# Conditioning tiles in the norm gaps of a four-layer trunk: ordered behind the last product and dealt out anew, with another order of the first inputs

## The chip, the cores and the metric

The kernel runs on one core of a Trainium2 chip. The metric is the device time of one execution in microseconds (us); the time given for a kernel is the median of several runs.

## The reference: what is computed

A decoder trunk of four layers over 256 tokens of width 1024 in float32. Each layer has a token mixer (layers 0 and 3: gMLP; layer 1: latent attention, MLA; layer 2: HGRN2, a gated linear recurrence) and a causal depthwise-convolution feed-forward network. Both are wrapped in adaptive norms whose shift, scale and gate come from one conditioning vector `c`:

```python
c_act = jax.nn.silu(c)
for i in range(DEPTH):
    mod = c_act @ ada_w[i] + ada_b[i]
    sh1, sc1, g1, sh2, sc2, g2 = jnp.split(mod, 6, axis=-1)
    h = modulate(rmsnorm(x, mix_norm_g[i]), sh1, sc1)
    ...
    x = x + (1.0 + g1)[:, None, :] * y
    h = modulate(rmsnorm(x, ffn_norm_g[i]), sh2, sc2)
    x = x + (1.0 + g2)[:, None, :] * conv_ffn(h, ff_w_up[i], ff_conv_w[i], ff_conv_b[i], ff_w_down[i])
return rmsnorm(x, final_g)
```

## The kernel before

**Products.** All weights stream from HBM in tiles of 1 MB (`raw`, five buffers, issued on SyncE's queue, SP). ScalarE (ACT) casts each half of a tile to a rounded part `wh` (L210), VectorE (DVE) takes the rest `wl` (L213), and TensorE (PE) makes three matmuls for each product (L243 to L245): high times high, and two cross terms. The activations are split likewise into `hh` and `hlo` (L599, L600).

**Stages.** Each layer runs a mixer (`mix`; in the gMLP its parts are `v`, `u` and `go`, in the HGRN mixer the projections, the levels `lev` and the output part `hout` that ends in the product `wo`), then `up` and `dn` of the feed-forward network. Between two stages lies a norm gap, eight in all, counted here from 0: gap 0 is go to up of layer 0, gap 1 is dn of layer 0 to the MLA mixer, gap 2 MLA's wo to up of layer 1, gap 3 dn to the HGRN mixer, gap 4 HGRN's wo to up of layer 2, gap 5 dn to the gMLP of layer 3, gap 6 its go to up. In a gap the last products go through the gate and the residual (`gated`, `x`: L522, L523, with the gate broadcast in `gx`), the root of the squares (`ss`, ACT, then a reciprocal on DVE, L459), the scaling (`gx`, L467 to L470), 16 transposes on PE (`xt`, L478), and the modulation on DVE (`nt`, L487, with the scale in `amul` and the shift in `mod`); only then can the next stage's first product run.

**Conditioning.** The six vectors of each layer, `mod`, are units (layer, u) with u = 0 to 5 for shift, scale and gate of the mixer norm, then of the feed-forward norm. Each unit is four tiles of 1 MB. Units in the list `ADA_P` are made on PE (`adaps`, L324: eight matmuls a tile, 16 records in the trace, since each is recorded twice), units in `ADA_D` on DVE (`adaw`, L349: two reductions over 128x1024 a tile). Units (0,0) and (0,1) come first, column by column (`adaf`, L371).

**What sets the order.** Every engine runs its instructions in the order in which the program's recording layer put them. The table `RATE` gives, for each stage, how many p and d tiles are loaded for every weight tile used; `pacing` (L413) runs a tile two weight tiles after its load. In the last `GAPW` = 7 weight tiles of a stage no p tile is run; up to `GAPS[gap]` of them are kept for the gap, where `modulated` (L491) runs them after the first transposes have been recorded. `need(l, u)` (L406) is the backstop: at a gap it runs, at once and in order, every tile up to the unit that the norm needs, whatever is left of it; `gate_load` (L278) calls it for the gate units, and then sends the gate through DRAM (`gate<-grow`, four small transfers) to be broadcast (`gx<-gate`). With `issue_after` the code holds one instruction behind another in the recorded order; `state["chain"]` does that for the casts and conditioning steps that must not come ahead of the root.

**The start.** x (two halves) goes first on SP's queue, `cin` (the conditioning vector) first on ACT's; twelve warm-up matmuls of 128x128 run on PE; then the first conditioning column `adaf`, the first transposes `xt`, and the products `v` column by column, in the order of the string `FIRST`.

## Time and profile before

| | |
|---|---|
| median of three runs | 1352.13 us (1352.03 to 1352.72) |
| profiled execution | 1353.27 us, of which the span of the trace 1351.2 us |
| mean granted clock of PE | 0.993 |
| PE busy | 1316.6 us, 97% |
| DVE busy | 1112.7 us, 82% |
| ACT busy | 773.5 us, 57% |
| moved by DMA | 330.68 MB, 245 GB/s mean |

Times in the trace are us from the start of the span. A timeline's row gives start, duration, engine, line of the kernel, operation, output and inputs, shapes, and in brackets the idle time of the engine just before, with what ended it. Matmuls are pipelined, so that the durations of neighbours overlap: start to start is what counts. In a window's row the last three columns are the granted clock (1.00 is full), the share of the 16 DMA engines, and GB/s.

### The profile page before, as it was taken

Reading aid. Unit: us, or ns where it says so; the run is one execution under the profiler, and the core shown is the slowest. Engines: PE = TensorE matmul, PEld = TensorE weight load, DVE = VectorE, ACT = ScalarE, POOL = GpSimd, SP = SyncE. Lnnn points to the kernel's source line nnn. Section 1 sums busy time; section 2 is a strip of 40 time slices with the busy share of each in tenths; the row PEclk is TensorE's granted clock in tenths of the full one; section 3 lists DMA queues with packets and bytes.
Section 4 is the critical chain, followed back from the end, with each engine's and each line's share of the span. In section 5 each row is a group of like instructions: output and inputs, shape, how many; then the busy total and the mean of one; then the engine's idle time right before and its main releaser. Section 6 shows DMA issues by size and latency. Waiting matters only on the chain.

```text
span 1351.2 us, 24627 instructions
## 1 busy us (share of the span) xinstructions
PE 1316.6 (97%) x10092; PEld 1192.5 (88%) x10092; DVE 1112.7 (82%) x1818; ACT 773.5 (57%) x1212; POOL 17.3 (1%) x27
## 2 busy tenths in 40 slices
PE   8999989999989999999999999999999999999997
PEld 6799789998777799998897879999878998899986
DVE  5699788888888789999889988988985964888854
ACT  3764366665366566654675647665455644666643
POOL 0100000000000000000000000000001000000000
PEclk8999999999999999999999999999999999999999
DMA  9868945557986466498675575558977445254550
GB/s 378 349 235 318 403 185 187 213 193 267 424 333 244 172 219 244 166 360 359 236 295 190 219 305 189 214 192 317 369 297 259 168 166 216 98 204 179 198 197 32
DMA packets 49160, 330.68 MB, mean 245 GB/s; under 512 B 6548, under 2 KB 7572, under 8 KB 10134
## 3 DMA queue, kind: packets, MB, share of 16 engines
q1 hardware_dynamic: 47888, 327.40, 63.7%
q10 hardware_dynamic: 1160, 1.71, 0.4%
q8 instruction: 79, 1.29, 0.4%
q14 instruction: 33, 0.27, 0.1%
HBM read 328.01 MB, written 1.08 MB: 244 GB/s over the span
## 4 chain that ended last, share of the span: by engine, by line
PE 85%; DVE 9%; ACT 3%; issue 1%; DMA 1%; ACTq 0%; DVEq 0%
PE up L245 12%; PE up L243 12%; PE up L244 12%; PE dn L243 5%; PE dn L245 5%; PE dn L244 5%; PE u L244 2%; PE u L243 2%; PE u L245 2%; DVE wl L213 2%; PE v L243 2%; PE v L244 2%; PE v L245 2%; PE go L243 2%; PE go L244 2%; PE go L245 2%
## 5 line engine op out<-in xcount | busy, mean ns | idle before, releaser
L210 ACT CAST wh<-raw 128x1024 fp32r<-128x1024 f32 x418 | 432.8, 1048 | 324.0 <-PE up L244 110.9
L213 DVE TENSOR_TENSOR wl<-raw,wh 128x1024 fp32r<-128x1024 f32 x418 | 507.2, 1225 | 84.6 <-ACT wh L210 83.8
L245 PE MATMUL up<-hh,wl 128*128 128x256 f32 x1408 | 397.8, 283 | 0.9 <-DVE wl L213 0.9
L243 PE MATMUL up<-hh,wh 128*128 128x256 f32 x1408 | 397.7, 284 | 0.0
L244 PE MATMUL up<-hlo,wh 128*128 128x256 f32 x1408 | 397.3, 283 | 0.1
L245 PEld LDWEIGHTS up<-hh,wl 128*128 128x128 f32 x1408 | 270.4, 192 | 1.3 <-DVE wl L213 1.3
L243 PEld LDWEIGHTS up<-hh,wh 128*128 128x128 f32 x1408 | 270.0, 192 | 0.6 <-issue 0.4
L244 PEld LDWEIGHTS up<-hlo,wh 128*128 128x128 f32 x1408 | 270.1, 192 | 0.3 <-DVE hlo L600 0.3
L349 DVE CUSTOM_DVE_ANT_0 adaw<-adaw,cbc,prm 128x1024 f32<-128x1024 f32 x120 | 151.3, 1282 | 0.3 <-DMA adaw<-adad 0.3
L244 PE MATMUL dn<-wl,gh 128*128 128x512 f32 x352 | 137.0, 389 | 0.0
L245 PE MATMUL dn<-wh,gl 128*128 128x512 f32 x352 | 136.8, 389 | 0.0
L243 PE MATMUL dn<-wh,gh 128*128 128x512 f32 x352 | 134.7, 390 | 0.5 <-DVE y L1217 0.5
L1215 ACT ACTIVATE y<-up,cwb 128x256 f32<-128x256 f32 x176 | 99.0, 562 | 58.1 <-DVE y L1217 57.9
L1216 DVE SCALAR_TENSOR_TENSOR y<-up,cwb,y 128x255 f32<-128x255 f32 x176 | 84.5, 480 | 34.0 <-ACT y L1215 33.5
L1217 DVE SCALAR_TENSOR_TENSOR y<-up,cwb,y 128x254 f32<-128x254 f32 x176 | 84.1, 478 | 1.5
L243 PEld LDWEIGHTS dn<-wh,gh 128*128 128x128 f32 x352 | 66.0, 188 | 15.2 <-issue 1.7
L245 PEld LDWEIGHTS dn<-wh,gl 128*128 128x128 f32 x352 | 66.1, 188 | 13.7
L244 PEld LDWEIGHTS dn<-wl,gh 128*128 128x128 f32 x352 | 66.1, 188 | 13.5
L243 PE MATMUL u<-hh,wh 128*128 128x256 f32 x256 | 74.0, 289 | 0.0
L245 PE MATMUL u<-hh,wl 128*128 128x256 f32 x256 | 72.4, 283 | 0.0
L244 PE MATMUL u<-hlo,wh 128*128 128x256 f32 x256 | 72.4, 283 | 0.0
L600 DVE TENSOR_TENSOR gl<-g,gh 128x256 fp32r<-128x256 f32 x88 | 37.1, 421 | 22.1 <-ACT gh L599 20.5
(332 smaller groups left out, 2060.4 us busy)
## 6 DMA issues: line engine op xcount, KB each, us to landing
raw<-up SPq DMA_DIRECT2D x88, 1024.0 KB
adaw<-adad SPq DMA_DIRECT2D x60, 1024.0 KB
raw<-dn SPq DMA_DIRECT2D x44, 1024.0 KB
adaw<-adap SPq DMA_DIRECT2D x28, 1024.0 KB
raw<-gmu SPq DMA_DIRECT2D x16, 1024.0 KB
raw<-gmo SPq DMA_DIRECT2D x16, 1024.0 KB
raw<-gmv SPq DMA_DIRECT2D x15, 1024.0 KB
adaf<-ada SPq DMA_DIRECT2D x8, 1024.0 KB
```

What stands on the lines that cost most here:

```text
L210: act.copy(wh[:, :w], raw[:, o : o + w])
L213: i = dve.tensor_tensor(wl[:, :w], raw[:, o : o + w], wh[:, :w].bitcast(F32), op=ALU.subtract)
L243: pe.matmul(ps, lh, rh, start=start, stop=False)
L244: pe.matmul(ps, lh, rl, start=False, stop=False)
L245: i = pe.matmul(ps, ll, rh, start=False, stop=stop)
L349: r = dve.tensor_tensor_reduce(raw[:, e, :], raw[:, e, :], cbc[:], 1.0, prm[:, c0 : c0 + 1], ALU.mult, ALU.add, mod[:, l, b : b + 1])
L600: b = dve.tensor_tensor(lo, src, h.bitcast(F32), op=ALU.subtract)
L1215: act.activation(y[:], ps[:, e, :], AF.Identity, bias=b, scale=w[2])
L1216: dve.scalar_tensor_tensor(y[:, 1:], ps[:, e, : S - 1], w[1], y[:, 1:], op0=ALU.mult, op1=ALU.add)
L1217: dve.scalar_tensor_tensor(y[:, 2:], ps[:, e, : S - 2], w[0], y[:, 2:], op0=ALU.mult, op1=ALU.add)
```

## The change

- **Deal.** The tables: `GAPS`, the number of p tiles for MLA (`MLA_ADA` 6 to 2), unit (3,2) from PE to DVE, and the rates. In layer 2 the d rates fall to 0.1, 0.0 and 0.1 in mix, lev and hout; in layer 3 they rise in mix, u and go and fall to 0 in dn.
- **Order in a gap.** In `modulated` the p tiles are held behind the last product matmul (`state["behind"]`).
- **Start.** 22 warm-up matmuls in place of 12, five more behind the first transposes; `cin` first on SP, one half of x on ACT's queue; the first `adaf` tile in two transfers; the squares of the two halves of x on the other engine each; the second half of the first weight tile is cast after hh, and the first `wl` taken after the first nt.
- **End.** The second output half is split at 640 of 1024 columns in place of 512.

```diff
-GAPS = [3, 2, 4, 3, 5, 3, 3, 0]
+GAPS = [3, 3, 3, 3, 2, 2, 2, 0]
...
-WARM = 12
+WARM = 22
+WARM2 = 5
...
-MLA_ADA = 6
+MLA_ADA = 2
...
-ADA_P = [(0, 5), (1, 2), (1, 3), (2, 4), (2, 5), (3, 2), (3, 5)]
+ADA_P = [(0, 5), (1, 2), (1, 3), (2, 4), (2, 5), (3, 5)]
...
-        ("mix", 2): (0.0, 0.4), ("lev", 2): (0.0, 0.25), ("hout", 2): (0.25, 1.05), ("up", 2): (0.0, 0.15),
+        ("mix", 2): (0.0, 0.1), ("lev", 2): (0.0, 0.0), ("hout", 2): (0.25, 0.1), ("up", 2): (0.0, 0.15),
...
     for t in range(2):
-        nc.sync.dma_start(x[:, t, :], A["x"][:, t, :])
-    cin = one.tile([P, 8], F32, name="cin")
-    nc.scalar.dma_start(cin[:], A["c"])
+        (nc.sync if t else nc.scalar).dma_start(x[:, t, :], A["x"][:, t, :])
...
+            if n == 0 and o and "first" in state:
+                es.enter_context(tc.issue_after(state["first"][1]))
             act.copy(wh[:, :w], raw[:, o : o + w])
-            if "sub1" in state:
-                es.enter_context(tc.issue_after(state["sub1"]))
+            if n == 0 and "first" in state:
+                es.enter_context(tc.issue_after(state["first"][0]))
             i = dve.tensor_tensor(wl[:, :w], raw[:, o : o + w], wh[:, :w].bitcast(F32), op=ALU.subtract)
...
-                for k in range(2):
-                    kc = 2 * i + k
-                    for j in range(4):
-                        pe.matmul(ps[32 * j : 32 * j + 32, :], crep(kc), raw[:, k, j, :], start=kc == 0, stop=kc == KC - 1,
-                                  tile_position=(0, 32 * j))
+                with contextlib.ExitStack() as es:
+                    for ins in state["behind"]:
+                        es.enter_context(tc.issue_after(ins))
+                    for k in range(2):
+                        kc = 2 * i + k
+                        for j in range(4):
+                            pe.matmul(ps[32 * j : 32 * j + 32, :], crep(kc), raw[:, k, j, :], start=kc == 0, stop=kc == KC - 1,
+                                      tile_position=(0, 32 * j))
...
         xts = [turned(*i) for i in tiles[:3]]
+        state["behind"] = (state["mm"],)
         while loaded["p"]:
             ada_run("p")
         need(l, 1 + 3 * which)
+        state["behind"] = ()
...
+    def warm(n):
+        for i in range(n):
+            r = pe.matmul(adaps[:, 0, 0:P], onesw[:], onesw[:], start=True, stop=True)
+        return getattr(r, "ins", r)
+
+    warm(WARM)
...
-                                state.setdefault("sub1", modulate_chunk(l, 0, c, xt[0][:, c % 2, :])[0])
+                                ins = modulate_chunk(l, 0, c, xt[0][:, c % 2, :])
+                                if c == 0:
+                                    state["first"] = ins
+                                    with tc.issue_after(state["xt"]):
+                                        firsts["pe"] = warm(WARM2)
```

**Gap 0 on PE.** Ahead of the change PE had the three conditioning tiles (`adaw_5_0` to `adaw_5_2`, unit (0,5)) among the last products `go` of layer 0. Where they begin:

```order
L245 MATMUL go_1503<-wh_1024_1666,yl_869 128x512
L324 MATMUL adaps<-adaw_5_0_1514,cact 32x256 x8
L324 MATMUL adaps<-adaw_5_1_1556,cact 32x256 x8
L324 MATMUL adaps<-adaw_5_2_1594,cact 32x256
L243 MATMUL go_1500<-wh_0_1698,yh_868 128x512
L243 MATMUL go_1501<-wh_0_1698,yh_868 128x512
```

With the change, the end of go:

```order
L248 MATMUL go_1518<-wh_1024_1753,yl_884 128x512
L330 MATMUL adaps<-adaw_5_0_1529,cact 32x256 x8
L330 MATMUL adaps<-adaw_5_1_1571,cact 32x256 x8
L330 MATMUL adaps<-adaw_5_2_1609,cact 32x256 x8
L488 MATMUL xt<-ident,gx 128x128 x16
L246 MATMUL up_1946<-hh,wh_0_1774 128x256
```

All 24 conditioning matmuls have moved from among the products, of which 48 still followed, to between the last product and the transposes.

**Gap 4 on DVE.** Before, from the root of the second token half to the modulation of up's first columns (layer 2):

```order
L459 RECIPROCAL ss<-ss 128x1
L469 TENSOR_SCALAR gx<-x,ss 128x512
L487 TENSOR_SCALAR nt<-xt,amul,mod 128x256 x2
L600 TENSOR_TENSOR hlo<-nt,hh 128x256
L487 TENSOR_SCALAR nt<-xt,amul,mod 128x256
```

The same place with the change; `adaw_3_0` to `adaw_3_3` are the four tiles of unit (2,3), the shift of this norm, and each pair of rows of `adaw` and `mod` is one reduction and the reading of its sum:

```order
L469 RECIPROCAL ss<-ss 128x1
L355 ISA adaw_3_0_8871,mod<-adaw_3_0_8871,cbc,prm 128x1024
L355 ISA mod 128x1
L479 TENSOR_SCALAR gx<-x,ss 128x512
L355 ISA adaw_3_0_8871,mod<-adaw_3_0_8871,cbc,prm 128x1024
L355 ISA mod 128x1
L355 ISA adaw_3_1_8875,mod<-adaw_3_1_8875,cbc,prm 128x1024
...
L355 ISA adaw_3_3_8883,mod<-adaw_3_3_8883,cbc,prm 128x1024
L355 ISA mod 128x1
L498 TENSOR_SCALAR nt<-xt,amul,mod 128x256 x2
L615 TENSOR_TENSOR hlo<-nt,hh 128x256
```

Eight reductions stand between the root and the first nt; before, they were done in the HGRN mixer.

**The gate of the HGRN residual on SP.** Before, SP sent the gate row of unit (2,2) (`gate20`) between two weight tiles of the projections, and the broadcast `gx_8794` much later. With the change both stand at the end of the output part, behind two tiles of up and four or five of conditioning:

```order
L346 DMA adaw2_2_3_8730<-adad 128x2048
L189 DMA raw119_8746<-up 128x2048
L189 DMA raw120_8780<-up 128x2048
L346 DMA adaw2_3_0_8871<-adad 128x2048
L316 DMA adaw2_5_1_8644<-adap 128x2048
L316 DMA adaw2_5_2_8696<-adap 128x2048
L346 DMA adaw2_3_1_8875<-adad 128x2048
L278 DMA gate20_8739<-grow_8737 8x32 x4
L346 DMA adaw2_3_2_8879<-adad 128x2048
L292 DMA gx_8744<-gate20_8739 128x1024
```

The last tile of unit (2,2) itself, `adaw2_2_3`, now comes only ahead of these.

More of the change, by code (lines that the diff above doesn't have):

```diff
@@ L46 @@
 HOLD = (3, 4)
-ADA_P = [(0, 5), (1, 2), (1, 3), (2, 4), (2, 5), (3, 2), (3, 5)]
+ADA_P = [(0, 5), (1, 2), (1, 3), (2, 4), (2, 5), (3, 5)]
 ADA_D = [(0, 2), (0, 3), (0, 4), (1, 0), (1, 1), (1, 4), (1, 5), (2, 0), (2, 1), (2, 2), (2, 3), (3, 0), (3, 1),
-         (3, 3), (3, 4)]
+         (3, 2), (3, 3), (3, 4)]
 RATE = {("mix", 0): (0.05, 0.4), ("u", 0): (0.1, 0.9), ("go", 0): (0.35, 0.7), ("up", 0): (0.05, 0.05),
-        ("dn", 0): (0.0, 0.87), ("mix", 1): (1.85, 0.6), ("up", 1): (0.0, 0.2), ("dn", 1): (0.0, 0.93),
-        ("mix", 2): (0.0, 0.4), ("lev", 2): (0.0, 0.25), ("hout", 2): (0.25, 1.05), ("up", 2): (0.0, 0.15),
-        ("dn", 2): (0.0, 1.09), ("mix", 3): (0.0, 0.5), ("u", 3): (0.0, 0.3), ("go", 3): (0.0, 0.5),
-        ("up", 3): (0.35, 0.0), ("dn", 3): (0.0, 0.76)}
+        ("dn", 0): (0.0, 0.87), ("mix", 1): (1.05, 0.6), ("up", 1): (0.0, 0.2), ("dn", 1): (0.0, 0.93),
+        ("mix", 2): (0.0, 0.1), ("lev", 2): (0.0, 0.0), ("hout", 2): (0.25, 0.1), ("up", 2): (0.0, 0.15),
+        ("dn", 2): (0.0, 0.5), ("mix", 3): (0.0, 0.6), ("u", 3): (0.0, 0.5), ("go", 3): (0.0, 0.7),
+        ("up", 3): (0.0, 0.0), ("dn", 3): (0.0, 0.0)}
 MAGIC = 12582912.0
@@ L125, in build @@
     prm = one.tile([P, NPRM], F32, name="prm")
+    cin = one.tile([P, 8], F32, name="cin")
+    nc.sync.dma_start(cin[:], A["c"])
     for t in range(2):
-        nc.sync.dma_start(x[:, t, :], A["x"][:, t, :])
-    cin = one.tile([P, 8], F32, name="cin")
-    nc.scalar.dma_start(cin[:], A["c"])
+        (nc.sync if t else nc.scalar).dma_start(x[:, t, :], A["x"][:, t, :])
     ident = one.tile([P, P], F32, name="ident")
@@ L171, in want @@
         plan.extend(aps)
-    state = {"dma": 0, "conv": 0, "use": 0, "ahead": 2, "chain": (), "left": 99, "tag": "raw", "p": 0.0, "d": 0.0, "gap": 0, "rate": {"p": 0.0, "d": 0.0}}
+    state = {"dma": 0, "conv": 0, "use": 0, "ahead": 2, "chain": (), "behind": (), "left": 99, "tag": "raw", "p": 0.0, "d": 0.0, "gap": 0, "rate": {"p": 0.0, "d": 0.0}}
     raws = []
@@ L363, in ada_first @@
         raw = wp.tile([P, KC, 4, 64], F32, tag="raw", name=f"adaf{c}", bufs=NRAW)
-        nc.sync.dma_start(raw[:].rearrange("p a b c -> p (a b c)"), A["ada0"][l, c])
+        rawf = raw[:].rearrange("p a b c -> p (a b c)")
+        for o in (0, 1024) if c == 0 else ():
+            nc.sync.dma_start(rawf[:, o : o + 1024], A["ada0"][l, c, :, o : o + 1024])
+        if c:
+            nc.sync.dma_start(rawf, A["ada0"][l, c])
         ps = misc(f"adaf{c}", (P, 64))
@@ L477, in turned @@
             for t in range(2):
-                pe.transpose(ps[:, e, t * P : t * P + P], cur["gx"][:, t, (c + e) * P : (c + e) * P + P], ident[:])
+                i = pe.transpose(ps[:, e, t * P : t * P + P], cur["gx"][:, t, (c + e) * P : (c + e) * P + P], ident[:])
+        state["xt"] = getattr(i, "ins", i)
         return ps
@@ L546, in finish @@
             s = slice(512 * f, 512 * f + 512)
+            if t:
+                s = slice(640 * f, 640 + 384 * f)
             if t == 0:
@@ L1250, in build @@
         act.activation(cbc[:], cbc[:], AF.Silu)
-    warm = misc("warmup", (P, P))
-    for i in range(WARM):
-        pe.matmul(warm[:], onesw[:], onesw[:], start=True, stop=True)
+    def warm(n):
[3 more added lines that the diff above has]
+    warm(WARM)
     cur["gx"] = big("gx", (P, 2, D))
@@ L1258, in build @@
         act.activation(sm("warm", 1)[:], epsc[:], AF.Sqrt)
-    act.activation(sq0[:, 0, :], x[:, 0, :], AF.Square, accum_out=ss0[:, 0:1])
-    dve.tensor_tensor_reduce(sq0[:, 1, :], x[:, 1, :], x[:, 1, :], 1.0, 0.0, ALU.mult, ALU.add, ss0[:, 1:2])
+    dve.tensor_tensor_reduce(sq0[:, 0, :], x[:, 0, :], x[:, 0, :], 1.0, 0.0, ALU.mult, ALU.add, ss0[:, 0:1])
+    act.activation(sq0[:, 1, :], x[:, 1, :], AF.Square, accum_out=ss0[:, 1:2])
     for t in range(2):
```

## The prediction

> **What bounds the kernel now.** I read the busy table of the page and its chain of waits first, then the windows and the timeline of the places that the change touches.
>
> ```profile
> PE 1316.6 (97%) x10092; PEld 1192.5 (88%) x10092; DVE 1112.7 (82%) x1818; ACT 773.5 (57%) x1212; POOL 17.3 (1%) x27
> PE 85%; DVE 9%; ACT 3%; issue 1%; DMA 1%; ACTq 0%; DVEq 0%
> ```
>
> TensorE is busy for 97% of a 1351.2 us span, and the chain that ends last is 85% TensorE. Its idle time is 1351.2 - 1316.6 = 34.6 us. So a change can win only by (a) closing idle time, (b) taking TensorE work off the path into idle time or to another engine, (c) avoiding time at half clock. The places are the start, and the norm gaps between a last product and the next first one. All sums are made on the profiled run, 1353.27 us (span plus 2.07); the median of the three runs is 1352.13, and I carry the difference over to it.
>
> **The start.** Two windows (columns: stretch, length, PE, PEld, DVE, ACT and POOL busy, clock, DMA share, GB/s), then TensorE's timeline:
>
> ```profile
> 10.20:13.39 3.19, 1.20 (x16) 0.72 (x5) 2.34 (x7) 2.40 (x3) 0.00 (x0) 0.50 1.04 434
> 13.39:17.03 3.64, 3.64 (x9) 2.87 (x10) 1.54 (x2) 0.00 (x0) 0.00 (x0) 0.50 1.01 421
> ```
> ```profile
> 1.05 5.49 PE L1253 MATMUL warmup<-ones 128*128 128x128 f32 x24 [1.05 <-POOL epsc L151]
> 9.24 1.11 PE L371 MATMUL adaf<-adaf,cact 128*32 128x64 f32 x64 [2.69 <-ACT gx L470]
> 13.39 1.65 PE L243 MATMUL v<-wh,hh 128*128 128x512 f32 x3 [1.99 <-ACT hh L599]
> 17.47 0.40 PE L244 MATMUL v<-wl,hh 128*128 128x512 f32 x1
> 17.70 0.40 PE L245 MATMUL v<-wh,hlo 128*128 128x512 f32 x1
> ```
>
> After the warm-up TensorE idles 2.69 us, and the first twelve products run at half clock. At full clock a product of this shape comes 0.23 us after the last (17.47 to 17.70), so twelve take 2.8 us instead of 13.39 to 17.93, 4.5 us: 1.7 us at stake, and part of the wait of 1.99 ahead of them, since hh moves ahead of the second wh cast on ACT. The 22 matmuls of the new warm-up are 44 records; at the 5.49 / 24 = 0.229 us of before they would end at 11.1, at full clock by half of that from some point on, about 9. But the transfers are full, at a share of 1.04 and 1.01 and 421 GB/s in the two windows, and the same bytes stand ahead of each conditioning tile (1 MB costs 2.5 us). TensorE that is ready 2.7 us earlier meets the next tile's landing. I take -1.0 us (bounds -2.7 and +0.3).
>
> **Gap 0, go to up of layer 0.** TensorE's timeline:
>
> ```profile
> 157.78 2.35 PE L324 MATMUL adaps<-adaw,cact 128*32 128x256 f32 x34
> 161.17 0.63 PE L324 MATMUL adaps<-adaw,cact 128*32 128x256 f32 x6
> 166.49 0.64 PE L324 MATMUL adaps<-adaw,cact 128*32 128x256 f32 x8
> 176.64 0.55 PE L478 MATMUL xt<-ident,gx 128*128 128x128 f32 x3 [3.85 <-DVE gx L467]
> 180.27 0.56 PE L243 MATMUL up<-hh,wh 128*128 128x256 f32 x1
> ```
>
> All 48 records (24 matmuls, three tiles) stand ahead of the last product, where they cost 2.35 + 0.63 + 0.64 = 3.6 us of busy TensorE, 3.4 net of overlap; then TensorE idles 3.85 us. The order of after puts all 24 behind the last product, in that idle time. The windows show what else goes:
>
> ```profile
> 177.50:180.80 3.30, 3.22 (x15) 3.22 (x16) 2.63 (x8) 2.15 (x5) 0.00 (x0) 0.50 0.00 0
> 180.90:184.30 3.40, 3.40 (x30) 3.40 (x30) 3.38 (x7) 3.09 (x6) 0.00 (x0) 1.00 0.01 2
> ```
>
> The transposes run at half clock. In gap 2, where conditioning tiles fill the time ahead, they don't: ```profile
> 464.55 2.26 PE L478 MATMUL xt<-ident,gx 128*128 128x128 f32 x16 [0.18 <-DVE gx L467]
> ```
>
> Sixteen take 2.26 us there, 0.14 each, against 0.55 / 3 = 0.18 and more here, and the first up products lose some as well: another 0.8 us, an estimate. Gap 0: -4.2 us (bounds -5.0 and -3.4).
>
> The Trainium skill, "TensorE: Matmul & The Clock Gate", Part 4, says that transposes don't count as busy for the clock. By it the clock would have stayed at half beyond 180.8, another 1.7 us to win here and as much in the other two gaps that stand idle. The row of 180.90 at 1.00, after 3.3 us that were mostly transposes, speaks against it, and I give it no chance beyond the range.
>
> **dn0 and gap 1.** Records of conditioning tiles alone, then the timeline:
>
> ```profile
> 358.00:371.00 13.00, 1.93 (x32) 0.94 (x32) 0.00 (x0) 1.00 1.01 421
> 380.00:462.00 82.00, 8.60 (x106) 3.14 (x106) 0.89 (x2) 1.00 0.68 264
> ```
> ```profile
> 375.07 0.61 PE L478 MATMUL xt<-ident,gx 128*128 128x128 f32 x3 [3.70 <-DVE gx L467]
> ```
>
> Sixteen matmuls (1.93 us) come off the path into 3.70 us of idle time, with 0.8 of clock as in gap 0: 2.7 us. Against that, one more tile of 1 MB has to land here where the DMA share is already 1.01: 2.5 us on a stream whose dn tiles are needed in turn, of which I count 0.8, and eight matmuls of a fourth tile stay behind the first products, 0.5. Net -1.4 us (bounds -2.7 and +0.3).
>
> **The MLA mixer.** Between 380 and 462 us 106 records, 53 matmuls, cost 8.60 us; after has 15 there. 38 x 8.60 / 53 = 6.2 us of TensorE's work goes. How much of it hid a wait for softmax scaling cannot be read while TensorE is busy:
>
> ```profile
> 380.00:462.00 82.00, 81.71 (x606) 67.62 (x604) 65.32 (x148) 48.46 (x107) 0.74 (x3) 1.00 0.68 264
> 450.00:462.00 12.00, 12.00 (x60) 9.59 (x58) 6.83 (x13) 5.36 (x11) 0.00 (x0) 1.00 0.53 205
> 420.00:430.00 10.00, 9.76 (x60) 7.69 (x60) 9.56 (x32) 6.52 (x24) 0.00 (x0) 1.00 1.00 415
> ```
>
> Where DVE is at 9.56 of 10 and TensorE does little but fill, a tile less only makes a wait visible; where DVE is at 6.83 of 12 it is a gain. I take 30%: -1.8 us (bounds -6.2 and 0). Gap 2 then holds 24 matmuls where it held 19: +0.2.
>
> **The HGRN mixer and gap 4.** This is the term that decides. DVE's timeline of gap 4, an undisturbed pair of conditioning steps, and TensorE's:
>
> ```profile
> 670.90 1.28 DVE L349 CUSTOM_DVE_ANT_0 adaw<-adaw,cbc,prm 128x1024 f32<-128x1024 f32 x1
> 672.11 1.28 DVE L349 CUSTOM_DVE_ANT_0 adaw<-adaw,cbc,prm 128x1024 f32<-128x1024 f32 x1
> 810.02 0.16 DVE L459 RECIPROCAL ss<-ss 128x1 f32<-128x1 f32 x1 [1.12 <-ACT ss L458]
> 810.22 0.49 DVE L469 TENSOR_SCALAR gx<-x,ss 128x512 f32<-128x512 f32 x1
> 811.27 0.99 DVE L487 TENSOR_SCALAR nt<-xt,amul,mod 128x256 f32<-128x256 f32 x2 [0.57 <-PE xt L478]
> ```
> ```profile
> 806.40 0.39 PE L245 MATMUL wo<-wh,hyl 128*128 128x512 f32 x1
> 813.88 0.36 PE L243 MATMUL up<-hh,wh 128*128 128x256 f32 x1
> ```
>
> With hgrn rates near 0, unit (2,3), the shift of this very norm, is not done by then: after's order has its eight DVE steps between that reciprocal and the first nt. 8 x 1.21 = 9.7 us in front of every nt. From the last wo: reciprocal at 810.02 - 806.40 = 3.6, gx 0.5, burst 9.7, so nt at 13.8 where it stood at 4.9; nt to product was 1.0 us where TensorE waited for nothing else:
>
> ```profile
> 658.80 1.00 DVE L487 TENSOR_SCALAR nt<-xt,amul,mod 128x256 f32<-128x256 f32 x2 [0.42 <-PE xt L478]
> 659.84 0.38 PE L243 MATMUL hf<-hh,wh 128*128 128x256 f32 x1
> ```
>
> So the first up product comes at 14.8 where it came at 813.88 - 806.40 = 7.5: +7.4 us. TensorE has 16 matmuls and 16 transposes to do in that time, some 2.80 x 16 / 24 + 2.26 = 4.1 us (the 2.80 from gap 5, below), and idles the rest, over twice the 3.85 us that took the clock down in gap 0: half clock when the products start costs 0.3 (the little of it that fell on products in gap 0) to 1.8 us (the first window of products at the start, 3.64 us, half of it); I take 1.0. With 0.6 for wl casts and gates that queue behind the burst: +9.0 us (bounds +7.0 and +12). The Trainium skill, same page, Part 1, gives the clock's window as about 3.4 us; by it the loss is at most 1.7, which would leave the sum as it is.
>
> What was removed from the mixer to get there paid little. DVE is the full engine between 750 and 772, with no conditioning step in it, and before that it waits for ACT; in the output part TensorE waits 1.4 + 1.2 us (the last two rows, from the list of waits):
>
> ```profile
> 750.00:772.00 22.00, 21.25 (x250) 20.38 (x252) 21.88 (x23) 12.65 (x15) 0.00 (x0) 1.00 0.59 227
> PE hst L1169 <- ACT osq L1162: 1.4, 1, 1.4
> PE obc L1180 <- DVE osd L1172: 1.2, 1, 1.2
> ```
>
> I take -0.6 (bounds -2.6 and 0).
>
> **The rest.** In dn2 one tile (eight matmuls, 2.80 / 3 = 0.93 us) now stands before the last products, where gap 5 held all three:
>
> ```profile
> 1001.19 2.80 PE L324 MATMUL adaps<-adaw,cact 128*32 128x256 f32 x48
> 1153.79 2.61 PE L478 MATMUL xt<-ident,gx 128*128 128x128 f32 x11 [2.36 <-DVE gx L469]
> ```
>
> +0.8 (bounds +0.3 and +1.2), DVE's relief there counted. Gap 6 gets 16 matmuls, 1.9 us, where TensorE waits 2.36: about 0, as is unit (3,2), eight more DVE steps in layer 3 and 32 matmuls less in layer 2, and the split of the last output: +0.1 together (bounds -0.8 and +0.8).
>
> **Sum.** -1.0 - 4.2 - 1.4 - 1.8 + 0.2 + 9.0 - 0.6 + 0.8 + 0.1 = +1.1 us: 1354.4 for a profiled run, 1353.2 against the median of 1352.13. Gains of 9 us in the first half, given back in one gap.
>
> **The rivals.** (1) *The tiles of the MLA mixer were on the path.* TensorE at 81.71 of 82 us speaks for it, DVE at 9.56 of 10 against. Then -6.2 instead of -1.8: 1348.8, faster. (2) *The gate comes late*, which ends slower. The same rates leave unit (2,2), the gate of this residual, to the output part too; its gate row goes out behind the transfers of the order's SP piece, and gx behind that. The analogue of before:
>
> ```profile
> 792.97 0.20 DVE L272 STREAM_TRANSPOSE grow<-gcol 128x32 f32<-128x32 f32 x1
> 793.20 1.31 SPq L275 DMA_DIRECT2D gate<-grow  x4
> 802.75 0.69 DVE L522 TENSOR_TENSOR gated<-wo,gx 128x512 f32<-128x512 f32 x1 [1.77 <-PE wo L245]
> ```
>
> So gx is issued at 795 or later and needed at 802.75, behind up to four tiles at 2.5 us: landing between 797 and 806. It decides from 802.75 on; at 806.2 it costs 3.5 us: 1356.7. (3) *The warm-up doesn't do what it says:* at 0.229 us a record it ends at 11.1, past the 9.24 at which adaf could start, and the start gains nothing: 1354.2.
>
> **How the numbers follow.** Chances: forecast 0.40, rival 1 0.30, rival 2 0.22, rival 3 0.08. No change is within 0.2% (2.7 us, about what a measurement of this kernel can tell): 1349.4 to 1354.8. The forecast's own range, 1350.5 to 1356.5, lies mostly in there, with a third above; rival 1 is mostly below; rival 2 mostly above. Faster: 0.03 + 0.24 + 0.01 = 0.28. Slower: 0.12 + 0.18 + 0.02 = 0.32. Same: 0.40. The range reaches 1.4 us past rival 1 and 0.9 past rival 2: 1347.4 to 1357.6.
>
> **What would show it.** Last go to first up in gap 0 at 5.1 to 5.5 us at clock 1.00, with no conditioning record before the last go; eight adaw steps in a row on DVE in gap 4 and some 15 us from last wo to first up, with a half-clock window; first v at about 12 us and then TensorE waiting for DMA. Wrong would be: gap 4 under 11 us, or a residual of the HGRN mixer in which gated waits for DMA, or an MLA mixer shorter by 4 us or more.

## The result: 0.5% slower, and two terms of the sum far too small

| | before | after |
|---|---|---|
| median | 1352.72 us of five runs (1352.03 to 1353.32) | 1359.4 us of four runs (1358.08 to 1360.56) |
| ratio | | 1.0050 [1.0034, 1.0066] |
| profiled execution, span | 1353.27, 1351.2 us | 1358.08, 1356.0 us |
| PE busy | 1316.6 us | 1313.9 us |

A fifth run of the changed kernel, at 1436.2 us with a clock of 0.847, was disturbed and is left out. The prediction was 1353.2 us, at most 1357.6; the kernel came out slower than that. From the changed kernel's page, the busy times and the chain that ended last:

```profile
PE 1313.9 (97%) x10058; PEld 1190.0 (88%) x10058; DVE 1124.3 (83%) x1832; ACT 773.5 (57%) x1212; POOL 19.5 (1%) x27
PE 80%; DVE 11%; DMA 3%; ACT 3%; issue 1%; SPq 0%; ACTq 0%; DVEq 0%
```

PE has 2.7 us less to do and the span is 4.8 us longer: its idle time went from 34.6 to 42.1 us. The chain has less of PE in it (85% before) and 3% of DMA and 3% of ACT. PE's list of waits (total, times, longest) says where:

```profile
PE up L246 <- ACT hh L614: 9.3, 2, 8.3
PE xt L488 <- DVE gx L477: 3.1, 4, 1.2
PE dn L246 <- ACT wh L213: 3.0, 2, 1.7
PE adaf L381 <- DMA adaf<-ada: 2.3, 3, 1.0
```

The second row stood at 8.0 before: that is what the new order took away. The first and the third are new, and ACT, which they name, is only the messenger in both. The last row is the start's: the first v comes at 12.56 us, and PE waits for conditioning tiles, as forecast. Stage by stage, by the starts of products in the two traces ("100th up" is the point at which 100 up products have gone, dn0 is dn of layer 0, cq the first product of MLA; negative is earlier, us):

| up to | before | after | step | forecast |
|---|---|---|---|---|
| 100th up of layer 0 (start, gap 0) | 192.61 | 187.28 | -5.3 | -5.2 |
| first cq (dn0, gap 1) | 378.70 | 372.90 | -0.5 | -1.4 |
| last wo of MLA | 461.69 | 452.30 | -3.6 | -1.8 |
| first up of layer 1 (gap 2) | 466.79 | 459.50 | +2.1 | +0.2 |
| last wo of HGRN | 806.40 | 799.16 | 0.0 | -0.6 |
| 100th up of layer 2 (gap 4) | 825.96 | 827.79 | +9.1 | +9.0 |
| last dn of layer 2 | 1000.87 | 1006.53 | +3.8 | +0.8 with gap 5 |
| end (gap 5, layer 3) | 1351.2 | 1356.0 | -0.9 | +0.1 |
| sum | | | +4.8 | +1.1 |

The sum is that of one execution, the fastest of the four; the ratio of all stands for about 6.8 us. The 2 us between them are not in these two traces. The traces of kernels that have the changed kernel's code in a stage show where single executions differ: from the 100th up to the last dn of layer 0 it takes 178.0 to 178.8 us in seven of them and 180.1 to 180.4 in the three (a_hold, a_keep2, a_mla6) that have a half-clock stretch of 3.41 us at 356; the HGRN mixer takes 151.7 to 151.9 us, or 152.8 to 153.0 with such a stretch in it; a_xt_behind has its last go of layer 0 1.2 us later than the changed kernel with the same code up to there. So a difference of about 1 us between two single traces proves nothing by itself.

**Gap 0**, PE's timeline with the change:

```profile
167.56 0.39 PE L248 MATMUL go<-wh,yl 128*128 128x512 f32 x1
167.88 2.80 PE L330 MATMUL adaps<-adaw,cact 128*32 128x256 f32 x48
171.80 0.77 PE L488 MATMUL xt<-ident,gx 128*128 128x128 f32 x5 [1.12 <-DVE gx L477]
174.14 0.39 PE L246 MATMUL up<-hh,wh 128*128 128x256 f32 x1
```

The 48 records lie behind the last go, where PE waited 3.85 us before and waits 1.12 now. The order is the forecast one. The gap itself is 6.6 us (7.9 before), not the 5.1 to 5.5 that I had named, and the first hundred up products take 13.1 us for 12.3; most of the gain lies ahead of the gap, where the 3.6 us among the products went.

**Gap 4**, the end of the residual and then DVE's timeline, and a window (PE, PEld, DVE, ACT, POOL, clock, DMA share, GB/s):

```profile
795.51 0.69 DVE L535 TENSOR_TENSOR gated<-wo,gx 128x512 f32<-128x512 f32 x1 [1.77 <-PE wo L248]
...
802.77 0.16 DVE L469 RECIPROCAL ss<-ss 128x1 f32<-128x1 f32 x1 [1.11 <-ACT ss L468]
802.85 1.27 DVE L355 CUSTOM_DVE_ANT_0 adaw<-adaw,cbc,prm 128x1024 f32<-128x1024 f32 x1
...
811.68 1.28 DVE L355 CUSTOM_DVE_ANT_0 adaw<-adaw,cbc,prm 128x1024 f32<-128x1024 f32 x1
...
812.88 0.99 DVE L498 TENSOR_SCALAR nt<-xt,amul,mod 128x256 f32<-128x256 f32 x2
```
```profile
804.58 0.98 PE L488 MATMUL xt<-ident,gx 128*128 128x128 f32 x7 [0.18 <-DVE gx L479]
813.91 0.58 PE L246 MATMUL up<-hh,wh 128*128 128x256 f32 x1 [8.35 <-ACT hh L614]
```
```profile
807.45:817.65 10.20, 3.74 (x16) 3.57 (x17) 10.18 (x20) 4.15 (x7) 0.00 (x0) 0.50 0.97 390
```

Eight reductions stand between the root and the first nt, PE idles 8.35 us, and the clock is at half for 10.2 us, from the burst into the first products. From the last wo (799.16) to the first up it is 14.75 us; I had said 14.8. The first row is rival 2's: the gate was there in time, and DVE waited for PE's wo, as before.

**dn2**, which I had taken for one tile's 0.9 us. SP's timeline before, where the gate row had gone out long ahead, at 827.54, and a dn tile followed the broadcast at once:

```profile
971.11 0.38 SPq L289 DMA_DIRECT2D gx<-gate  x1
971.58 0.39 SPq L188 DMA_DIRECT2D raw<-dn  x1
```

With the change, SP's timeline, then ACT's and PE's:

```profile
965.03 0.33 SPq L316 DMA_DIRECT2D adaw<-adap  x1
983.82 1.30 SPq L278 DMA_DIRECT2D gate<-grow  x4
986.03 0.34 SPq L292 DMA_DIRECT2D gx<-gate  x1
986.47 0.85 SPq L189 DMA_DIRECT2D raw<-dn  x2
```
```profile
994.30 2.00 ACT L213 CAST wh<-raw 128x1024 fp32r<-128x1024 f32 x2 [14.39 <-DMA raw<-dn]
```
```profile
981.47 1.07 PE L330 MATMUL adaps<-adaw,cact 128*32 128x256 f32 x16
...
995.40 1.19 PE L246 MATMUL dn<-wh,gh 128*128 128x512 f32 x4 [1.73 <-ACT wh L213]
```

The tile that now comes late (the last of unit (2,5)) is made at 981.47, and the gate row of that unit needs it. The gate's four small transfers stand in SP's queue ahead of the next dn tiles, and nothing goes out on SP between 965.4 and 983.8. The dn tiles behind them leave at 986.47, ACT has nothing to cast for 14.39 us (its longest wait for a dn tile here was 4.26 before), and PE runs dry.

**Gap 2**, DVE's timeline before, then DVE's and PE's with the change:

```profile
465.76 0.99 DVE L487 TENSOR_SCALAR nt<-xt,amul,mod 128x256 f32<-128x256 f32 x2 [0.42 <-PE xt L478]
```
```profile
457.77 0.45 DVE L297 STREAM_TRANSPOSE adat<-adaps 128x256 f32<-128x256 f32 x1 [1.82 <-PE adaps L330]
458.26 0.17 DVE L299 TENSOR_TENSOR mod<-adat,prm 128x8 f32<-128x8 f32 x1
```
```profile
455.61 0.63 PE L330 MATMUL adaps<-adaw,cact 128*32 128x256 f32 x6
456.17 0.98 PE L488 MATMUL xt<-ident,gx 128*128 128x128 f32 x7
457.08 0.63 PE L330 MATMUL adaps<-adaw,cact 128*32 128x256 f32 x6
```

Before, DVE waited only for the transposes. With the change the last conditioning matmuls of the gap run between the transposes and end at 457.7; DVE waits 1.82 us for them, and then still has the shift to make before nt.

**MLA and dn0.** Records of conditioning tiles between the first cq and the last wo:

```profile
372.90:452.30 79.40, 2.49 (x30) 0.89 (x30) 0.44 (x1) 1.00 0.65 249
```

8.60 - 2.49 = 6.1 us of PE's work went and the stretch got 3.6 us shorter: 59% of it was on the path, not 30%. In dn0 the extra 1 MB took more than I gave it (ACT's timeline):

```profile
353.25 1.99 ACT L213 CAST wh<-raw 128x1024 fp32r<-128x1024 f32 x2 [12.62 <-DMA raw<-dn]
```

### The profile page after: what moved, and what is told of

Read it like the earlier page. It is cut to its first block, busy times and chain, and to the rows that moved or that the text cites. A ratio compares the mean times of both kernels' runs of the same rounds, so it can differ in the third digit from the quotient of the medians.

```text
span 1356.0 us, 24579 instructions
## 1 busy us (share of the span) xinstructions
PE 1313.9 (97%) x10058; PEld 1190.0 (88%) x10058; DVE 1124.3 (83%) x1832; ACT 773.5 (57%) x1212; POOL 19.5 (1%) x27
## 3 DMA queue, kind: packets, MB, share of 16 engines
q8 instruction: 79, 1.29, 0.4%
## 4 chain that ended last, share of the span: by engine, by line
PE 80%; DVE 11%; DMA 3%; ACT 3%; issue 1%; SPq 0%; ACTq 0%; DVEq 0%
PE up L248 12%; PE up L246 12%; PE up L247 12%; PE dn L247 5%; PE dn L248 5%; PE dn L246 5%; DVE wl L216 2%; PE u L247 2%; PE u L246 2%; PE u L248 2%; PE go L246 2%; PE go L247 2%; PE go L248 2%; DMA adaf<-ada 1%; PE v L246 1%; PE v L247 1%
## 5 line engine op out<-in xcount | busy, mean ns | idle before, releaser
L246 PEld LDWEIGHTS up<-hh,wh 128*128 128x128 f32 x1408 | 270.4, 193 | 10.7 <-ACT hh L614 10.2
L355 DVE CUSTOM_DVE_ANT_0 adaw<-adaw,cbc,prm 128x1024 f32<-128x1024 f32 x128 | 163.4, 1297 | 1.3 <-DMA adaw<-adad 1.3
L247 PEld LDWEIGHTS dn<-wl,gh 128*128 128x128 f32 x352 | 66.1, 188 | 14.8 <-DVE wl L216 1.5
```

The lines of the kernel that those rows point to most:

```text
L246: pe.matmul(ps, lh, rh, start=start, stop=False)
L247: pe.matmul(ps, lh, rl, start=False, stop=False)
L355: r = dve.tensor_tensor_reduce(raw[:, e, :], raw[:, e, :], cbc[:], 1.0, prm[:, c0 : c0 + 1], ALU.mult, ALU.add, mod[:, l, b : b + 1])
```

## The experiments

| kernel | median, us | ratio to before [95%] |
|---|---|---|
| old HGRN rates on after (a_hold) | 1349.22 | 0.9976 [0.9967, 0.9985] |
| new HGRN rates on before (b_hnew) | 1363.88 | 1.0082 [1.0068, 1.0096] |
| five tiles in gap 4 (a_gap5) | 1358.20 | 1.0042 [1.0028, 1.0055] |
| four tiles in gap 1 (a_gap4_1) | 1357.32 | 1.0036 [1.0023, 1.0048] |
| two tiles in gap 1 (a_dn0) | 1357.16 | 1.0034 [1.0021, 1.0047] |
| gate row on another queue (a_gateq) | 1357.97 | 1.0036 [1.0024, 1.0049] |
| gap 2 in another order (a_xt_behind) | 1357.38 | 1.0027 [1.0016, 1.0038] |
| six p tiles in MLA (a_mla6) | 1359.84 | 1.0043 [1.0030, 1.0055] |
| PE kept busy in gap 4, bank of the small sums (a_keep) | 1366.11 | 1.0096 [1.0082, 1.0109] |
| the same, bank of a product (a_keep2) | 1357.11 | 1.0033 [1.0021, 1.0046] |
| order in the gaps alone, on before (b_behind) | 1347.13 | 0.9947 [0.9935, 0.9960] |
| start and end split alone, on before (b_start) | 1355.59 | 1.0016 [1.0007, 1.0025] |
| warm-ups alone, on before (b_warm) | 1355.28 | 1.0018 [1.0009, 1.0028] |
| input order and casts alone, on before (b_in) | 1354.32 | 1.0011 [1.0002, 1.0021] |
| 15 tiny matmuls at the start of before (b_pad) | 1356.25 | 1.0019 [1.0010, 1.0029] |
| repairs together (best1) | 1344.26 | 0.9933 [0.9921, 0.9946] |
| the same with the old start (best2) | 1345.84 | 0.9942 [0.9928, 0.9955] |
| best1 and two tiles in gap 1 (best3) | 1341.07 | 0.9910 [0.9897, 0.9924] |

The kernel before had medians of 1352.8 to 1353.8 us on these chips.

The time of the whole fell where it was expected in a_xt_behind, b_behind and best1. It was outside in a_hold (0.8 us below), b_hnew (1.9 above), a_gap5 (some 2 above), a_gap4_1 (2.3 above), a_mla6 (1.3 above), b_start (3.7 above), b_pad (0.75 above), best2 (0.6 above) and best3 (1.4 below), and by less than 0.5 us in b_warm and b_in; for the others a stretch was named, not the whole. What follows rests on the stretches.

**The burst in gap 4: old rates on after (a_hold), new rates on before (b_hnew).** a_hold:

```diff
-        ("mix", 2): (0.0, 0.1), ("lev", 2): (0.0, 0.0), ("hout", 2): (0.25, 0.1), ("up", 2): (0.0, 0.15),
+        ("mix", 2): (0.0, 0.4), ("lev", 2): (0.0, 0.25), ("hout", 2): (0.25, 1.05), ("up", 2): (0.0, 0.15),
```

b_hnew is the reverse edit on the kernel before.

> The changed kernel with one part undone: the d rates of the HGRN mixer as before (0.4, 0.25, 1.05), so that units (2,2) and (2,3) are done in the mixer and gap 4 has no burst on DVE. Theory (burst): from the last wo to the first up 5.1 to 7.5 us instead of 14.75, the hundredth up product about 9 us earlier, no half-clock window there, and 1350 to 1352 us in all against some 1359 of the changed kernel; the stall in dn2 stays. Rival (the work only moves): the sixteen DVE steps cost in the mixer what they saved in the gap, the last wo comes 3 us or more later, and the time stays above 1355.

> The kernel before with that one part alone: the new d rates of the HGRN mixer (0.1, 0.0, 0.1). Theory (burst): gap 4 from 7.5 to some 14.8 us and half clock at its end, 7.5 to 9.5 us slower than before, 1360 to 1362; the last wo within 1 us of before. Rival (the work only moves): the mixer is shorter by 3 us or more, and the whole at most 4 us slower.

a_hold: DVE's timeline has no reduction between root and nt,

```profile
804.17 0.16 DVE L469 RECIPROCAL ss<-ss 128x1 f32<-128x1 f32 x1 [1.12 <-ACT ss L468]
804.37 0.49 DVE L479 TENSOR_SCALAR gx<-x,ss 128x512 f32<-128x512 f32 x1
805.28 0.99 DVE L498 TENSOR_SCALAR nt<-xt,amul,mod 128x256 f32<-128x256 f32 x2 [0.42 <-PE xt L488]
```

gap 4 falls from 14.75 to 5.76 us, and the whole to below before. On the kernel before the rates alone make gap 4 14.99 us where it was 7.47. The burst theory is shown from both sides. In b_hnew the gate of the HGRN residual is late as well (DVE's timeline):

```profile
806.23 0.69 DVE L522 TENSOR_TENSOR gated<-wo,gx 128x512 f32<-128x512 f32 x1 [2.04 <-DMA gx<-gate]
```

But DVE waits 1.77 us at this place for PE in any case (before and after), and from this row to the last wo it is 3.4 us where it was 3.65: the late gate costs about 0.3 us, and the gap is 14.99 us for the 14.75 of the changed kernel. So rival 2 was near, and the same rates in another deal just bring it on.

**Where the late tile belongs (a_gap5, a_gap4_1).** `GAPS` gets 5 for 2 in gap 4, or 4 for 3 in gap 1:

```diff
-GAPS = [3, 3, 3, 3, 2, 2, 2, 0]
+GAPS = [3, 3, 3, 3, 5, 2, 2, 0]
```

> The changed kernel with five p tiles in gap 4 instead of two, as before: the last tile of the gate unit (2,5) then runs inside gap 4, where TensorE idles anyway, and not in dn2. Theory (queue): in dn2 the gate row's transfers no longer hold SP's queue for 18 us, ACT no longer waits 14 us for a tile of dn, and dn2 to gap 5 is 2.5 to 3.6 us shorter: about 1356. Rival (bandwidth): dn2 stalls because the transfers of its last tiles come at a share of 1.01 of the DMA engines; then dn2 keeps its wait of 1.7 us and the time stays within 1 us of the changed kernel.

> The changed kernel with four p tiles in gap 1 instead of three: the shift unit (1,3) is then finished two matmul groups earlier in gap 2, ahead of the transposes, and the tile of (2,5) that stood in dn2 is run in gap 4. Theory (late shift): gap 2 from 7.2 to 5.1 to 5.6 us because DVE no longer waits 1.8 us for the last tile's sums, gap 1 longer by at most 0.5; with the stall of dn2 gone too, 1354 to 1355. Rival (PE full): gap 2 is long because TensorE has 24 matmuls and 16 transposes to do there; then it stays at 7 us, since as many stand in it, and only dn2 gains.

In both the last tile of unit (2,5) is done before dn2, ACT has no wait for a dn tile there, and from the 100th up to the last dn of layer 2 it takes 175.13 and 175.12 us where after takes 178.74 and before 174.91. In a_gap5 gap 4 is shorter (12.34) and its first products are longer by as much, since two of the eight reductions now stand behind the first nt: gap and first products together are the same. The part of a_gap4_1's expectation on gap 2 failed: it stayed at 7.19 us, with the same 1.82 us wait of DVE, so the late shift there is no matter of which unit's tile comes last: `modulated` makes the shift only when every p tile of the gap has run.

**The queue (a_gateq).** The gate row and the broadcast of this one gate are issued on GpSimd's queue:

```diff
-            nc.sync.dma_start(row[:, j, :], r[32 * j : 32 * j + 8, :])
+            (nc.gpsimd if (l, which) == (2, 1) else nc.sync).dma_start(row[:, j, :], r[32 * j : 32 * j + 8, :])
...
```

> The changed kernel with one thing moved: the gate row and the gate's broadcast of dn2 are issued on GpSimd's queue instead of SP's. The late tile of (2,5) and all transfers stay. Theory (queue): SP sends the last tiles of dn at 965 to 975 us instead of 986, ACT no longer waits 14 us, and from the hundredth up product of layer 2 to the last dn 176 to 176.5 us instead of 178.7 (the tile's own 1.07 us on TensorE stays). Rival (bandwidth): the tiles land late whoever issues; 178.4 or more.

SP's timeline, then ACT's:

```profile
969.47 5.20 SPq L189 DMA_DIRECT2D raw<-dn  x2
```
```profile
985.60 1.05 ACT L213 CAST wh<-raw 128x1024 fp32r<-128x1024 f32 x1 [1.66 <-PE dn L248]
989.57 1.05 ACT L213 CAST wh<-raw 128x1024 fp32r<-128x1024 f32 x1 [2.92 <-PE dn L248]
```

The dn tiles leave at 969.47, 0.4 us after the last conditioning tile, ACT waits only for PE, and the stretch takes 176.38 us: 2.4 of the 3.8 us were the blocked queue. (Kernels that keep the blocked queue take 177.5 to 178.7 us there, so it is 1.2 to 2.4.) The rest is about the tile itself: the one longer wait, 2.92 for 1.66, is 1.26 us. The execution lost time in gap 1 (9.36 us for 6.96), which the edit doesn't touch, so the whole says little here.

**Gap 2 (a_xt_behind).** All p tiles of this gap are recorded, and `mod` stored, ahead of the transposes:

```diff
...
-        xts = [turned(*i) for i in tiles[:3]]
+        first = l == which == 1
+        if first:
+            state["behind"] = (state["mm"],)
+            while loaded["p"]:
+                ada_run("p")
+            need(l, 1 + 3 * which)
+        with contextlib.ExitStack() as es:
+            if first:
+                es.enter_context(tc.issue_after(state["pe"]))
+            xts = [turned(*i) for i in tiles[:3]]
```

> The changed kernel with another order in gap 2 alone: all 24 conditioning matmuls there stand ahead of the 16 transposes, and the shift of unit (1,3) is stored right behind its last tile. Theory (late shift): DVE reads the sums at about 455.5 instead of 457.8, gap 2 falls from 7.2 to 5.1 to 5.6 us, the rest stays: 1.6 to 2.1 us faster than the changed kernel, about 1357.5. Rival (PE full): 24 matmuls and 16 transposes need the gap; it stays at 6.5 us or more.

```profile
453.67 2.80 PE L330 MATMUL adaps<-adaw,cact 128*32 128x256 f32 x48
456.39 2.29 PE L489 MATMUL xt<-ident,gx 128*128 128x128 f32 x16
458.70 0.39 PE L246 MATMUL up<-hh,wh 128*128 128x256 f32 x1
```

PE's timeline runs through without a wait, and the gap is 5.35 us instead of 7.20, with the same 24 matmuls in it. a_mla6, below, shows the same from another side: there the shift is made in the mixer, the 24 matmuls stand where the changed kernel has them, and the gap is 5.98 us.

**MLA's tiles (a_mla6) and dn0's (a_dn0).** `MLA_ADA = 6` with the MLA layer's p rate at 1.85 for 1.05, and `GAPS` with 2 for 3 in gap 1:

```diff
-GAPS = [3, 3, 3, 3, 2, 2, 2, 0]
+GAPS = [3, 2, 3, 3, 2, 2, 2, 0]
```

> The changed kernel with the MLA mixer's p tiles as before (six and a rate of 1.85): 4 more tiles run inside the mixer, (1,3) is done there, and (2,5) by gap 3 to the HGRN mixer. Theory: the mixer is 3 to 3.6 us longer (the gain of the changed kernel in it goes), gap 2 is 2 us shorter, and the stall of dn2 is gone (3 us): 1357 to 1358.5. Rival (the tiles in the mixer are free): the mixer is at most 1 us longer, and the whole 4 us faster, 1355.

> The changed kernel with two p tiles in gap 1 instead of three, as before. Theory (transfers of dn0): one tile of 1 MB less is loaded ahead of the last tiles of dn, which land about 2.5 us earlier; from the hundredth up product of layer 0 to the last dn 176.3 us instead of 178.7. Rival (TensorE's order): 178 us or more, and the loss in dn0 has another cause.

With six tiles back in MLA its stretch takes 83.26 us (after 79.40, before 83.0): the tiles there were mostly on the path. The stall of dn2 is gone, too (175.1 us), and gap 2 is 1.2 us shorter, where 2 had been expected. The whole is no better for it: dn0 and the HGRN mixer are longer by 1.7 and 1.2 us in this execution, each with a half-clock stretch in it. With one tile less in gap 1 the stretch from the 100th up to the last dn of layer 0 is 176.30 us for 178.66. The wait of ACT for dn tiles is not gone but is cut from 12.62 to 8.29 us, and PE, which waited 1.8 us for dn's casts there with the change, has none of these waits left (ACT's timeline of a_dn0):

```profile
348.91 2.01 ACT L213 CAST wh<-raw 128x1024 fp32r<-128x1024 f32 x2 [8.29 <-DMA raw<-dn]
353.90 2.01 ACT L213 CAST wh<-raw 128x1024 fp32r<-128x1024 f32 x2 [2.98 <-DMA raw<-dn]
```

Two other kernels without that tile, b_behind and best3, take 176.29 us as well, so the tile costs 1.7 to 2.5 us, and about 4 in the three executions with a half clock there. Gap 2 pays 0.85 us of it back, since 32 matmuls now lie there.

**The clock in gap 4 (a_keep, a_keep2).** 36 idle matmuls of 128x128 ahead of the first nt, in the bank of the small sums (a_keep, `misc` for `acc`) or in one of the products' banks (a_keep2, shown):

```diff
+            if l == 2 and which == 1 and i == 0:
+                keep = acc("keep", (P, P))
+                for _ in range(36):
+                    pe.matmul(keep[:], onesw[:], onesw[:], start=True, stop=True)
```

> The changed kernel with 36 idle matmuls (their result is not used) on TensorE in gap 4, behind the transposes, so that it stays busy during the burst. Theory: the gap stays at 14.7 to 15 us, for DVE sets it; the half-clock window goes, and the first hundred up products take 13.1 us or less instead of 13.9: 0.8 to 1.8 us faster. Rival (the clock sets the gap): the gap itself gets shorter by 2 us or more.

> The changed kernel with 36 idle matmuls on TensorE in gap 4, this time into a bank that is free there (one of the four of the products), between the transposes. Theory: DVE sets the gap, which stays at 14.5 to 15 us, without a half-clock window; the first hundred up products take 12.1 to 13.1 us instead of 13.9. Rival (the clock sets the gap): the gap is 2 us or more shorter.

a_keep decides nothing: its matmuls waited 7.92 us for the bank, and then stood ahead of the products. In a_keep2 they ran in the idle time,

```profile
806.49 5.52 PE L518 MATMUL keep<-ones 128*128 128x128 f32 x48
811.85 0.82 PE L488 MATMUL xt<-ident,gx 128*128 128x128 f32 x6
814.49 0.38 PE L246 MATMUL up<-hh,wh 128*128 128x256 f32 x1 [1.82 <-ACT hh L618]
```

the gap stayed at 14.75 us and the first 100 products took 13.13 us for 13.88. So the half clock cost 0.75 us in this execution, and the gap is DVE's. How much it costs follows what part of the stretch lies on the products: 3.6 us of it cost 0.7 (a_dn0), 4.9 us 1.25 (a_gap4_1, a_gateq), 5.7 us 1.6 (a_mla6).

**The order alone (b_behind) and the start alone (b_start, b_warm, b_in).** Each is that part of the change's diff on the kernel before; b_start has the split of the last output with it.

> The kernel before with the order in the gaps alone: p tiles behind the last product, no other edit. Theory: gap 0 and the end of go 4.2 us shorter, dn0 and gap 1 up to 2.7 shorter less what its transfers take back, gap 2 about 0.1 either way: 1346 to 1349. Rival (the transfers of dn0 take it back): the tiles of dn land at the same time as before, so that at most 2 of these 6 us are left after gap 1, and the time stays above 1350.

> The kernel before with the start of the changed one (warm-ups, order of the first inputs, first casts, split of the last output) and nothing else. Theory (transfers bound the start): the first twelve v run at full clock from about 12 us, then TensorE waits for the next conditioning tiles, and by the last go 1.0 to 1.6 us are won: 1351.3 to 1351.9 if nothing downstream takes it back. Rival (the whole wait goes): 2.7 us or more won by the last go, about 1350.

> The kernel before with the warm-ups of the changed one alone (22, and five behind the first transposes). Theory (the new start is lost to later clock windows and the transfers): the first v run at full clock, 0.3 to 1 us won by the last go, and the whole within 2 us of before either way, with the differences in gap 1 and the HGRN mixer. Rival (the order of inputs costs the 2 us): not slower than before.

> The kernel before with the order of the first inputs and casts alone, without the new warm-ups. Theory: the first v start up to 0.9 us earlier but at half clock, by the last go nothing is won or lost by more than 0.5 us, and the whole is within 1 us of before. Rival (the order of inputs costs the 2 us): 1.5 us slower or more.

The order alone wins 6.0 us up to the first cq and still has 5.8 at the end (spans 1345.4 and 1351.2): the best single part of the change. (Gap 2 became 0.86 us longer by it, where 0.1 had been expected.) The new start brings the first up of layer 0 forward by 0.9 us in b_start, 1.3 in b_warm, and puts it back by 0.6 in b_in; all three end slower, by 0.1 to 0.2%. So the theory of b_start (1351.3 to 1351.9) failed in what comes later. It loses 1.05 us in MLA, at whose beginning it has a half-clock stretch of 6.83 us for the 3.41 of before. And with the warm-ups in (b_start, b_warm) time is lost some 650 us later, in the HGRN mixer, whose code they do not touch: from the last dn of layer 1 to the last wo it takes 152.6 and 154.4 us for 151.7. There PE stops among the small gram matmuls and waits for nothing that the profile shows. The two have the same stop, of 2.4 and 2.7 us from start to start; b_warm has a half-clock stretch of 3.41 us right behind it (at 747) and b_start none, which goes with the 1.7 us between them.

**Why an edit of the start costs time in the HGRN mixer (b_pad).** 15 matmuls of 16 columns behind the warm-up of the kernel before:

```diff
+    for i in range(15):
+        pe.matmul(warm[:, 0:16], onesw[:], onesw[:, 0:16], start=True, stop=True)
```

> The kernel before with 15 tiny products of 16 columns on TensorE after the start's last warm-up product, nothing else; they write a bank nobody reads. They cost below 0.5 us at the start. Theory (position in TensorE's instruction stream): the stretch from the last dn1 product to the last wo product is longer than before's 151.7 us, by 1 to 2.5 us, with a pause of over 2 us that waits for nothing among the tiny gram products, as in the two runs that have 15 more TensorE instructions ahead of it; time 1354 to 1355.5. Rival (the pause comes from the new start's own timing, not from the count): that stretch is 151.7 us within 0.3 and the time is 1353.0 within 0.5.

PE's timeline of b_pad, and of before at the same run of 128 records (64 matmuls, each recorded twice):

```profile
744.04 1.15 PE L1052 MATMUL gram<-qk 128*32 128x32 f32 x111
747.53 0.34 PE L1052 MATMUL gram<-qk 128*32 128x32 f32 x17 [2.34 <-issue]
```
```profile
744.07 1.30 PE L1052 MATMUL gram<-qk 128*32 128x32 f32 x128
...
747.85 0.39 PE L245 MATMUL hg<-hh,wl 128*128 128x256 f32 x1 [0.74 <-issue]
```

The pause has come back, and the stretch is 154.4 us, with a half-clock stretch of 3.41 us behind the pause as in b_warm. The inputs and their order are those of before. The start's timing is not quite: the half clock that before has from 10.20 to 17.03 is gone in b_pad, and its first up of layer 0 comes 1.0 us earlier. That this isn't what brings the pause is seen in the others: best2 starts with such a half clock and has the pause, best3 starts without one and has none. The place says more. Counting PE's matmul records from the program's start, the pause stands at record 5967 in before, b_start, b_warm, b_in and b_pad alike, whatever instruction that is, and another at 5584, in all twenty kernels; in best2, which has 30 records fewer than best1, there is one at 5711. These lie 128 records, or a multiple, from each other within one. A wait for DVE in the same run of grams, by contrast, stays with its instruction and moves between records 5464 and 5558 with the count ahead. A record comes with one of a weight load, so 128 are 256 instructions, and the page has a queue of instructions (packets, MB):

```profile
q8 instruction: 79, 1.29, 0.4%
```

1.29 MB in 79 packets is 16.3 KB each, and 2 x 10122 instructions in 79 packets are 256 each. This fits a program of PE that comes in blocks of 256 instructions: where a block ends with 111 gram records at about 10 ns each, PE would be through before the next has come; where a boundary falls 13 records behind the run, 0.74 us are left of the pause. The Trainium skill, "Runtime: NRT & Kernel Launch", section "Instruction fetch mechanics", has engines fetch in 16 KiB blocks of 256 instructions and calls the cost of a boundary mostly hidden; the trace agrees on the size, and here 2.34 us were not hidden. That the fetch is the cause is argued from place and size, and no run shows it; why the pause at record 5839 is 1.0 us in best1 and absent in best3 stays open.

**The repairs together (best1, best2, best3).** Old HGRN rates, a_xt_behind's order in gap 2, and `GAPS` with 3 in gap 4, so that the late tile is done before dn2. best2 has the old start and the old end; best3 has one tile less in gap 1:

```diff
-GAPS = [3, 3, 3, 3, 2, 2, 2, 0]
+GAPS = [3, 2, 3, 3, 3, 2, 2, 0]
```

> The changed kernel with three causes mended: d rates of the HGRN mixer as before, three p tiles in gap 4 (so that no tile of (2,5) is left for dn2), and in gap 2 the tiles ahead of the transposes. Theory (three stalls that add up): 10 + 3 + 1.9 us under the changed kernel, 1344 to 1345.5. Rival (they share a bound): 1347 or more.

> The same three mended causes, the new deal and the new order in the gaps, but the start of the kernel before. Theory (the start wins little and the transfers take it back): within 1 us of the same kernel with the new start, either way. Rival (the new start is a loss of 2 us, as it was alone): 1.5 to 2.5 us faster than with it.

> The changed kernel with the old rates of the HGRN layer, three tiles instead of more in gap 4, gap 2 with its p tiles ahead of the transposes (these three alone gave 1344.3 us), and now also the conditioning tile that stood between dn0's and cq's stages moved out of gap 1 into gap 2 (two tiles in gap 1). Theory (transfers): from the 100th up0 product to the last dn0 product 178.7 us falls to about 176.3, gap 2 grows by about 0.9 us, so the whole comes out about 1.5 us below 1344.3, at 1342.5 to 1343.5. Rival (the time comes back elsewhere: a tile is worth the same wherever it lies): 1344.3, with dn0 shorter by 2.4 us and another stretch longer by as much.

best1 is faster than both kernels, with gap 2 at 5.35 and gap 4 at 5.76 us. best2 is 1.6 us slower, of which its trace has 1.2 in the HGRN mixer, with a pause of 2.13 us of the kind above; so this pair doesn't settle what the new start is worth by itself. Up to the last go of layer 0 the two differ by 0.01 us. best3, from the 100th up to the last dn of layer 0, takes 176.29 us for best1's 178.71; the gaps give back 1.3 of it, MLA is 0.5 shorter and the HGRN mixer 1.3. best1 has there the pause of 1.0 us and a half-clock stretch of 3.41 us, best3 neither; a_gateq, with such a stretch and no pause at 5839, takes 153.03 us as best1 does, so that the 1.3 us go with the clock and are no gain of the edit. best3 is 0.9% faster than before.

## Why the prediction was wrong

**Start and gap 0: right** in the sum (-5.3 for -5.2). The order alone gives 3.9 of it (b_behind), for the 4.2 taken. What the start gives is less certain: 1.4 by this pair, 0.9 in b_start, nothing between best1 and best2.

**Gap 4: right** in mechanism and size (+9.1 for +9.0). The 1.0 taken for the clock was 0.75 by a_keep2, and 0.7 to 1.6 over the executions. The half clock lasted 10.24 us, not the one stretch of about 3.5 us by which its cost was bounded; the size held because only 3.8 us of it lay on the products.

**dn0 and gap 1: sign right, size off** (-0.5 for -1.4). The extra 1 MB that lands in dn0 costs 2.4 us (a_dn0), near the whole 2.5 us of a tile at full DMA; I had counted a third (0.8).

**MLA: sized too low** (-3.6 for -1.8). I read the share on the path from DVE's load, and took 30% where 59% was right. The truth lies two fifths of the way to rival 1. A PE at 81.71 of 82 us should have weighed more than a DVE near full in one part.

**Gap 2: failed** (+2.1 for +0.2). "Gap 2 then holds 24 matmuls where it held 19" counted PE's work and not what the last of them releases: the shift that DVE needs before nt. Where the last of them stands, and not PE's work, is most of the cost: with the same 24 matmuls the gap takes 5.35 us when they stand ahead of the transposes (a_xt_behind), 5.98 when the shift needs none of them (a_mla6), and 7.20 as it is.

**dn2: failed, and without this the result would lie inside the range** (+3.8 for +0.8). The step of "The rest" says that one tile "now stands before the last products", and prices it by its eight matmuls. It did not follow what waits for that tile: the gate row, four transfers that SP must issue ahead of the next dn tiles. I had drawn just this chain for the gate of the HGRN residual (rival 2), where it didn't bite, and did not ask it again for the gate of unit (2,5), a few lines further in my own sum. The queue is up to 2.4 of it, the tile the rest (a_gateq); with the tile in an earlier gap it is all gone (a_gap5, a_gap4_1).

**HGRN and layer 3** were off by 0.6 and 1.0, in opposite directions. The errors of MLA and gap 2 cancelled; dn0's and dn2's did not. The range had +1.2 as the worst of dn2. Its upper end was 5.5 us above before: the pair of traces (+4.8) is still inside it, the medians (+6.7) are not. So the 3.0 us of dn2 and the 2 us that other executions lose were both needed to leave it, and for those 2 us the causes are seen only in part (half-clock stretches in dn0 and the HGRN mixer).

## What to carry to other kernels

A step that is moved late has to be followed through every queue to the last thing that waits for it: a transfer that waits at the head of an issuing engine's queue holds back all the bulk transfers behind it (here for 18.5 us), and the price is theirs, not its own. In these runs, work that fills an idle gap was near free where it stood ahead of the step that the gap waits for, and cost 2 us where the way to the first product led through its last piece. When a small edit moves time in a far stage whose code is the same, look whether the count of instructions ahead has changed, and where the half-clock stretches lie.
